# An encoder on one core: the weights' hi parts moved from 64 to 192 bytes past a multiple of 256, and the v projection in 256-column products

## The chip, the core and the metric

The kernel runs on one core of a Trainium2 chip. The metric is the time on the device in microseconds (us), the median of several executions. The core has engines that work side by side: TensorE (PE in the profile, and PEld for its weight loads) multiplies a stationary operand of 128x128 with a moving operand of up to 512 columns and adds into PSUM; VectorE (DVE) and ScalarE (ACT) work elementwise; SyncE (SP) issues the transfers from memory (HBM) into the on-chip memory (SBUF). SBUF has 128 partitions; a byte offset below is always an offset within a partition.

## The reference

Two encoder layers on 256 tokens of width 2048, in float32. The first mixes tokens by a gated short convolution, the second by attention with three groups of dilated windows; each is followed by a gated MLP of width 5632 with a convolution of width 3. Cut to what matters:

```
for i in range(2):
    h = rmsnorm(x, mix_norm_g[i])
    x = x + (short_conv_mixer(h, ...) if i == 0 else dilated_attention_mixer(h, ...))
    h = rmsnorm(x, ffn_norm_g[i])
    u = dwconv3(h @ w_up, conv_w, conv_b)      # 2048 -> 2 * 5632
    a, b = split(u, 2)
    x = x + (silu(a) * b) @ w_down             # 5632 -> 2048
return rmsnorm(x, final_norm_g)

# attention: qkv = h @ w_qkv, 3 groups x (q, k, v) x 16 heads x 128;
# per group softmax(q k^T / sqrt(128) - slope * distance) v, the groups mixed by their denominators
```

Nearly all of the work is in the products with weight matrices: 2048 x 6144 and 2048 x 2048 in the first mixer, 2048 x 18432 and 2048 x 2048 in attention, 2048 x 11264 and 5632 x 2048 in each MLP.

## The kernel before

**Products in two parts.** PE multiplies in a rounded float32 form (F32R). To keep float32's accuracy, each operand is split into a hi part, the rounded value, and a lo part, the rest: `split` (L80) lets ACT copy the source into hi and DVE subtract hi from the source into lo. A product of two split operands is hi·hi + hi·lo + lo·hi. An activation tile (`h`, `a`, `y`, `o`) holds 512 columns per block of 128 channels: 256 tokens of hi (T = 256), then 256 tokens of lo.

**Most products** have the weights as the stationary operand. `mm` (L102) issues two products per block k: L108 multiplies the weights' hi part with all 512 columns of the activation, and L109 the weights' lo part with the 256 hi columns. The results stand in a PSUM tile of 512 columns, whose halves are added afterwards (`gathered`, L117). PE loads the stationary operand anew for every product, so such a pair has two loads: hi for L108, lo for L109. `mm1` (L98) is the same for the first weights of the program, `last` (L245) for the last projection's end; its last output block takes three products of 256 columns instead (L254 to L256), which all add into the same 256 columns.

**The weight tile.** `load_w` (L86) has SP load up to 16 blocks of 128x128 into `raw`, and splits them eight at a time into a tile `w2` of W2 columns; four such tiles are in turn. Where the hi and the lo part begin in it is set by the constants at the top, in elements of 4 bytes:

```
W2 = 2 * 8 * P + 64
HI = 16
LO = 8 * P + 64
LOV = 0
LOS = 9 * P + 64
HIV = 4 * 2 * P + 16
```

P is 128. HI and LO are for `load_w`, HI and LOS for the first weights in `short_conv` (L204), LOV and HIV for the v units. A `w2` tile is 8448 bytes, 33 x 256, and the pools lay every weight tile, every raw tile and the activations at a multiple of 256 bytes. So the hi parts begin 64 bytes past a multiple of 256 (16 elements), the lo parts at a multiple (LO is 4352 bytes, LOV 0). Only the small tiles of the pool "temps" (`tmp`, `e`, `sq`) lie 64 past one, by a spare tile of TPAD elements ahead of them.

**The v units** (`v_unit`, L361) have it the other way round: the activations `h` are stationary, and the weights move, 256 output channels (two heads) at a time. For each block k and each half i of the tokens there were two products: L380 multiplies the hi part of `h` with 512 columns, which an access pattern `both` collects from 256 columns of the weights' lo part and 256 of their hi part, and L381 multiplies the lo part of `h` with the weights' hi part and adds it to the second half of the PSUM tile. For `both` the two parts must lie as far apart (HIV) as half of the pattern's length. At the end of a unit ACT scales the first half into `tmp` (L389), and DVE scales the second half and adds `tmp` (L391). There are 24 v units, each with 16 blocks and 2 halves: 768 pairs.

**The order of work.** The stages follow one another: the short convolution (48 + 720 pairs for its first projection, 256 for its second), the first MLP (88 units of 16 pairs for w_up, and 64 units of 11 for w_down, chunk by chunk), attention, the second MLP. In attention, for each two heads, there are three v units, then twelve q/k units (`qk_unit`, 16 pairs each, 1536 in all), and between these units one waiting task at a time of earlier heads: scores (L413 to L415, L427), softmax, transposes (L446) and the products with v (L464, L469). The order of instructions on each engine is that of the code; a planner adds the semaphores. Four PSUM tiles of 512 columns are in turn, so PE can go on while ACT and DVE empty a finished one.

Of the kernel before, what the change touches and what calls it, by code (L numbers as in the profile page):

```python
# [10 lines left out]
F32 = mybir.dt.float32  # L11
F32R = mybir.dt.float32r
AF = mybir.ActivationFunctionType
ALU = mybir.AluOpType
AX = mybir.AxisListType

P = 128
T = 256
D = 2048
KT = D // P  # L20
# [10 lines left out]
TPAD = 16  # L31

W2 = 2 * 8 * P + 64
HI = 16
LO = 8 * P + 64
LOV = 0
LOS = 9 * P + 64
HIV = 4 * 2 * P + 16
QSCALE = float(P) ** -0.5


# [1 line left out]
def encoder_kernel(ctx: ExitStack, tc: tile.TileContext, xT, gs, scw, fcw, dist, w_first, w_in, w_so, w_v, w_qk, w_ao, w_up, w_dn, out):  # L43
# [3 lines left out]
    pe, dve, act = nc.tensor, nc.vector, nc.scalar  # L47
# [3 lines left out]
    tp = ctx.enter_context(tc.tile_pool(name="temps", bufs=2))  # L51
# [5 lines left out]
    rc = cp.tile([P, 2], F32, name="rc")  # L57
    x = cp.tile([P, KT, T], F32, name="x")
    h = cp.tile([P, KT, 2 * T], F32R, name="h")
# [20 lines left out]
    def split(hi, lo, src):  # L80
        ins = act.copy(hi, src)  # L81
        dve.tensor_sub(lo, src, f32(hi))  # L82
        return ins


    def load_w(src, n):  # L86
# [3 lines left out]
        for k0 in range(0, n, 8):  # L90
            m = min(8, n - k0)
            w2 = wp.tile([P, W2], F32R, name="w2", tag="w2", bufs=4)
            hi, lo = (w2[:, z : z + 8 * P].rearrange("p (k c) -> p k c", k=8) for z in (HI, LO))
            split(hi[:, :m, :], lo[:, :m, :], raw[:, k0 : k0 + m, :])
# [19 lines left out]
    def new_ps():  # L114
        return pp.tile([P, 2 * T], F32, name="ps", tag="ps", bufs=4)
# [66 lines left out]
    def short_conv():  # L182
        with tc.tile_pool(name="sc", bufs=1) as sp:
# [13 lines left out]
            for n in (1, 1, 2, 2, 3, 3, 2, 1, 1):  # L197
# [6 lines left out]
                w2 = sp.tile([P, LOS + 9 * P], F32R, name="w2s", tag="w2s", bufs=2)  # L204
                w2 = [w2[:, z : z + 9 * P].rearrange("p (k c) -> p k c", k=3) for z in (HI, LOS)]
                ins = split(w2[0][:, :n, :], w2[1][:, :n, :], raw[:, :n, :])
# [134 lines left out]
    def attention():  # L341
        with tc.tile_pool(name="att", bufs=1) as sp:
# [9 lines left out]
            def norms():  # L352
                rms()
                dve.tensor_copy(rp.rearrange("p (i m) -> p i m", i=2), rr.rearrange("p (m i) -> p i m", i=2))
                dve.tensor_scalar_mul(rq, rp, QSCALE)
                for i in range(2):
                    ps = pp.tile([P, 2 * T], F32, name="stat", tag="s", bufs=2)
                    pe.transpose(ps[:, :P], rp[:, i * P : (i + 1) * P], ident)
                    dve.tensor_copy(rc[:, i : i + 1], ps[:, 0:1])

            def v_unit(hp, g):  # L361

                first = hp == 0 and g == 0
                if g == 0:
                    v = sp.tile([P, 2, 2, T], F32R, name="v", tag="v0", bufs=2)
                else:
                    v = sp.tile([P, 2, T], F32, name="v", tag=f"v{g}", bufs=2)
                ps = [new_ps(), new_ps()]
                for k0 in range(0, KT, 8):
                    raw = wp.tile([P, 8, T], F32, name="rawv", tag="raw", bufs=RAW)  # L370
                    nc.sync.dma_start(raw, w_v[3 * hp + g, :, k0 * T : (k0 + 8) * T])
                    for k1 in range(k0, k0 + 8, 4):
                        w2 = wp.tile([P, W2], F32R, name="w2v", tag="w2", bufs=4)
                        lo, hi = (w2[:, z : z + 4 * T].rearrange("p (k c) -> p k c", k=4) for z in (LOV, HIV))
                        split(hi, lo, raw[:, k1 - k0 : k1 - k0 + 4, :])
                        both = w2[:, : 2 * HIV].rearrange("p (z c) -> p z c", z=2)
                        for k in range(k1, k1 + 4):
                            c = (k - k1) * T
                            for i in range(2):
                                pe.matmul(ps[i], h[:, k, i * P : (i + 1) * P], both[:, :, c : c + T], start=k == 0, stop=False)  # L380
                                pe.matmul(  # L381
                                    ps[i][:, T:], h[:, k, T + i * P : T + (i + 1) * P], hi[:, k - k1, :],
                                    start=False, stop=k == KT - 1,
                                )
                if first:
                    norms()
                for i in range(2):
                    tmp = tp.tile([P, T], F32, name="tmp", tag="tmp")
                    act.mul(tmp, ps[i][:, :T], rc[:, i : i + 1])  # L389
                    e = tp.tile([P, T], F32, name="e", tag="e0") if g == 0 else v[:, i, :]  # L390
                    dve.scalar_tensor_tensor(e, ps[i][:, T:], rc[:, i : i + 1], tmp, op0=ALU.mult, op1=ALU.add)  # L391
                    if g == 0:
                        split(v[:, i, 0, :], v[:, i, 1, :], e)
                vs[hp, g] = v
# [85 lines left out]
            for hp in range(H // 2):  # L480
                for g in range(G):
                    v_unit(hp, g)
                    step()
                for hd in (2 * hp, 2 * hp + 1):
                    for g in range(G):
                        qk_unit(hd, g, 0)
                        step()
                        qk_unit(hd, g, 1)
                        step()
                        tasks.append(lambda hd=hd, g=g: scores(hd, g))  # L490
                    tasks.append(lambda hd=hd: (softmax(hd, 0), softmax(hd, 1)))
                    tasks.append(lambda hd=hd: transposes(hd, 0))
                    tasks.append(lambda hd=hd: transposes(hd, 1))
                    tasks.append(lambda hd=hd: pv(hd))
            first = []
            for j in range(2):
                w = load_w(w_ao[j], KT)
                ps = new_ps()
# [5 lines left out]
            for j in range(KT):  # L504
                if j < 2:
                    ps, w = first[j]
                    mm(ps, w, o, range(KT - 1, KT))
                else:
                    w = load_w(w_ao[j], KT)
                    ps = new_ps()  # L510
# [90 lines left out]
```

## Time and profile before

| | |
|---|---|
| median of three runs | 2794.36 us |
| the three runs | 2794.18, 2794.36, 2823.95 us |
| the profiled execution: its own time | 2770.87 us |
| its span, first to last instruction | 2768.8 us |
| mean granted TensorE clock | 0.999 |
| DMA, share of 16 engines (SP's queue) | 53.1% |
| read from HBM | 514.76 MB, 187 GB/s over the span |

In a row of groups one reads the line of the kernel, the engine, the operation, output<-inputs by the program's names, the sizes and the count; behind the bar the busy time in us, the mean duration of one in ns, and the time that the engine was idle just before them with what ended it. PE's durations overlap, since a matmul's end is modelled and the next one starts before it; what one matmul really takes of PE's time is the distance from its start to the next start. A row of the timeline has the start in us, the duration in us, and then the same names. A row of the windows has the window, its length, the busy time of each engine with the count in parentheses, the granted TensorE clock, the DMA share and GB/s.

### The profile page before, as it was taken

What the parts mean: (1) busy time and instruction counts of PE and PEld (TensorE: products, weight loads), DVE (VectorE), ACT (ScalarE), POOL (GpSimd) and SP (SyncE); (2) the same over time, 40 slices, a digit from 0 to 9 for tenths busy, and PEclk for the clock granted to TensorE, in tenths of its full rate; (3) what the DMA queues carried; (4) which work ended last, traced back from release to release, by engine and by line L of the source; (5) the groups of instructions that cost most, each with busy time, mean ns of one, the idle gap of its engine ahead of it and who ended that gap; (6) DMA issues with size and microseconds to landing.
All of it is one profiled execution on the core that took longest, in us unless ns stands there. A gap on an engine that the chain in (4) does not pass through costs nothing.

```text
span 2768.8 us, 40538 instructions
## 1 busy us (share of the span) xinstructions
PE 2750.9 (99%) x16223; PEld 2432.0 (88%) x16223; DVE 1995.9 (72%) x3080; ACT 1502.1 (54%) x2335; POOL 0.7 (0%) x6
## 2 busy tenths in 40 slices
PE   9999999999999999999999999999999999999998
PEld 7888888888888888888888888888888888888887
DVE  7777788877868868655665666566788886877866
ACT  6454566655655556444444444444566655655655
POOL 0000000000000000000000000000000000000000
PEclk9999999999999999999999999999999999999999
DMA  7555555546555456544545454545455546556554
GB/s 251 207 188 197 198 188 193 198 167 215 191 183 210 171 189 221 186 177 168 182 171 176 171 182 168 177 173 179 171 195 189 195 170 220 189 176 218 177 183 144
DMA packets 79821, 519.48 MB, mean 188 GB/s; under 512 B 9104, under 2 KB 10256, under 8 KB 28816
## 3 DMA queue, kind: packets, MB, share of 16 engines
q1 hardware_dynamic: 79488, 516.37, 53.1%
q8 instruction: 127, 2.08, 0.3%
q14 instruction: 62, 0.51, 0.1%
q10 hardware_dynamic: 144, 0.52, 0.0%
HBM read 514.76 MB, written 2.10 MB: 187 GB/s over the span
## 4 chain that ended last, share of the span: by engine, by line
PE 99%; DMA 1%; DVE 0%; ACT 0%; SPq 0%; issue 0%; DVEq 0%; ACTq 0%
PE ps L108 57%; PE ps L109 29%; PE ps L380 6%; PE ps L381 3%; PE ot L469 1%; PE s L427 1%; PE pt L446 1%; PE ot L464 0%; DMA raw<-in_w_first 0%; DMA raw<-in_w_in 0%; DVE x L288 0%; PE s L415 0%; PE s L413 0%; PE s L414 0%; DVE w2s L82 0%; PE stat L169 0%
## 5 line engine op out<-in xcount | busy, mean ns | idle before, releaser
L108 PE MATMUL ps<-h,w 128*128 128x512 f32 x5072 | 1748.6, 392 | 0.3 <-ACT w L81 0.3
L109 PE MATMUL ps<-h,w 128*128 128x256 f32 x5072 | 1406.8, 277 | 0.0
L82 DVE TENSOR_TENSOR w<-raw,w 128x1024 fp32r<-128x1024 f32 (+1 forms) x954 | 1080.7, 1133 | 359.3 <-ACT w L81 341.7
L81 ACT CAST w<-raw 128x1024 fp32r<-128x1024 f32 (+1 forms) x954 | 934.7, 980 | 523.9 <-PE ps L109 420.4
L108 PEld LDWEIGHTS ps<-h,w 128*128 128x128 f32 x5072 | 952.2, 188 | 200.3 <-ACT w L81 0.6
L109 PEld LDWEIGHTS ps<-h,w 128*128 128x128 f32 x5072 | 954.7, 188 | 0.7 <-DVE w L82 0.6
L108 PE MATMUL ps<-a,w 128*128 128x512 f32 x1397 | 475.3, 389 | 0.0
L119 ACT COPY tmp<-ps 128x256 f32<-128x256 f32 x479 | 177.5, 371 | 471.1 <-PE ps L109 471.1
L109 PE MATMUL ps<-a,w 128*128 128x256 f32 x1397 | 385.6, 276 | 0.0
L121 DVE TENSOR_TENSOR e<-ps,tmp 128x256 f32<-128x256 f32 x479 | 201.9, 422 | 228.4 <-ACT tmp L119 228.4
L108 PEld LDWEIGHTS ps<-a,w 128*128 128x128 f32 x1397 | 262.2, 188 | 54.5
L380 PE MATMUL ps<-w2v,h 128*128 128x512 f32 x768 | 270.4, 396 | 0.0
L109 PEld LDWEIGHTS ps<-a,w 128*128 128x128 f32 x1397 | 262.2, 188 | 0.0
L381 PE MATMUL ps<-w2v,h 128*128 128x256 f32 x768 | 213.3, 278 | 0.0
L82 DVE TENSOR_TENSOR w2v<-rawv,w2v 128x1024 fp32r<-128x1024 f32 x96 | 117.5, 1224 | 99.8 <-ACT w2v L81 99.0
L380 PEld LDWEIGHTS ps<-w2v,h 128*128 128x128 f32 x768 | 144.1, 188 | 33.6
L81 ACT CAST w2v<-rawv 128x1024 fp32r<-128x1024 f32 x96 | 100.6, 1048 | 98.2 <-PE ps L381 69.8
L381 PEld LDWEIGHTS ps<-w2v,h 128*128 128x128 f32 x768 | 144.3, 188 | 0.0
L133 ACT ACTIVATE cv<-e,fcw_sb 128x256 f32<-128x256 f32 x176 | 105.7, 602 | 12.1 <-DVE e L128 11.9
L128 DVE TENSOR_TENSOR e<-e,rr 128x256 f32<-128x256 f32 x220 | 92.9, 424 | 6.8
L134 DVE SCALAR_TENSOR_TENSOR cv<-e,fcw_sb,cv 128x255 f32<-128x255 f32 x176 | 84.1, 479 | 8.0 <-ACT cv L133 8.0
L135 DVE SCALAR_TENSOR_TENSOR cv<-e,fcw_sb,cv 128x255 f32<-128x255 f32 x176 | 85.1, 484 | 6.1
(120 smaller groups left out, 1467.9 us busy)
## 6 DMA issues: line engine op xcount, KB each, us to landing
raw<-in_w_up SPq DMA_DIRECT2D x176, 1024.0 KB, 4.7
raw<-in_w_qk SPq DMA_DIRECT2D x96, 1024.0 KB, 4.7
raw<-in_w_dn SPq DMA_DIRECT2D x128, 704.0 KB, 4.0
rawv<-in_w_v SPq DMA_DIRECT2D x48, 1024.0 KB, 5.1
raw<-in_w_in SPq DMA_DIRECT2D x45, 1024.0 KB, 4.8
raw<-in_w_so SPq DMA_DIRECT2D x16, 1024.0 KB, 4.7
raw<-in_w_ao SPq DMA_DIRECT2D x16, 1024.0 KB, 4.8
raw<-in_w_first SPq DMA_DIRECT2D x3, 384.0 KB, 5.7
```

The lines of the kernel that those rows point to most:

```text
L81: ins = act.copy(hi, src)
L82: dve.tensor_sub(lo, src, f32(hi))
L108: pe.matmul(ps, hi[:, i, :], a[:, k, :], start=k == 0, stop=False)
L109: ins = pe.matmul(ps[:, :T], lo[:, i, :], a[:, k, :T], start=False, stop=k == n - 1)
L119: act.copy(tmp, ps[:, T:])
L121: dve.tensor_add(e, ps[:, :T], tmp)
L128: dve.tensor_mul(e, g, r)
L133: act.activation(c, e, AF.Identity, bias=w[:, 3:4], scale=w[:, 1:2])
L134: dve.scalar_tensor_tensor(c[:, 1:], e[:, : T - 1], w[:, 0:1], c[:, 1:], op0=ALU.mult, op1=ALU.add)
L135: dve.scalar_tensor_tensor(c[:, : T - 1], e[:, 1:], w[:, 2:3], c[:, : T - 1], op0=ALU.mult, op1=ALU.add)
L380: pe.matmul(ps[i], h[:, k, i * P : (i + 1) * P], both[:, :, c : c + T], start=k == 0, stop=False)
L381: pe.matmul(ps[i][:, T:], h[:, k, T + i * P : T + (i + 1) * P], hi[:, k - k1, :], start=False, stop=k == KT - 1,)
```

## The change

The hi parts in all weight tiles begin at element 48 in place of 16, which is 192 bytes past a multiple of 256; the lo parts of `load_w` and of the first weights stay at a multiple. In the v units' tiles the lo part begins at element 16 (64 bytes) and the hi part at 192 bytes past a multiple. The pattern `both` is gone: for each block and half there are three products of 256 columns, `h` hi with the weights' hi, `h` hi with the weights' lo, `h` lo with the weights' hi, all into the first 256 columns of the PSUM tile. The scaling at the end writes the result in one ACT operation, and DVE's scaling and sum fall away.

```
-HI = 16
+HI = 48
 LO = 8 * P + 64
-LOV = 0
 LOS = 9 * P + 64
-HIV = 4 * 2 * P + 16
+LOV = 16
+HIV = 4 * 2 * P + 48
...
-                        both = w2[:, : 2 * HIV].rearrange("p (z c) -> p z c", z=2)
                         for k in range(k1, k1 + 4):
-                            c = (k - k1) * T
                             for i in range(2):
-                                pe.matmul(ps[i], h[:, k, i * P : (i + 1) * P], both[:, :, c : c + T], start=k == 0, stop=False)
-                                pe.matmul(
-                                    ps[i][:, T:], h[:, k, T + i * P : T + (i + 1) * P], hi[:, k - k1, :],
-                                    start=False, stop=k == KT - 1,
-                                )
+                                a, b = (h[:, k, z + i * P : z + (i + 1) * P] for z in (0, T))
+                                pe.matmul(ps[i][:, :T], a, hi[:, k - k1, :], start=k == 0, stop=False)
+                                pe.matmul(ps[i][:, :T], a, lo[:, k - k1, :], start=False, stop=False)
+                                pe.matmul(ps[i][:, :T], b, hi[:, k - k1, :], start=False, stop=k == KT - 1)
                 if first:
                     norms()
                 for i in range(2):
-                    tmp = tp.tile([P, T], F32, name="tmp", tag="tmp")
-                    act.mul(tmp, ps[i][:, :T], rc[:, i : i + 1])
                     e = tp.tile([P, T], F32, name="e", tag="e0") if g == 0 else v[:, i, :]
-                    dve.scalar_tensor_tensor(e, ps[i][:, T:], rc[:, i : i + 1], tmp, op0=ALU.mult, op1=ALU.add)
+                    act.mul(e, ps[i][:, :T], rc[:, i : i + 1])
                     if g == 0:
                         split(v[:, i, 0, :], v[:, i, 1, :], e)
```

## The prediction

> **What bounds the kernel now.** I read the page first (busy shares, then the chain that ended last), then the groups by line with shapes kept apart, then the timeline of PE inside single units, because a busy PE is no measure of PE's pace. The page:
>
> ```profile
> PE 2750.9 (99%) x16223; PEld 2432.0 (88%) x16223; DVE 1995.9 (72%) x3080; ACT 1502.1 (54%) x2335; POOL 0.7 (0%) x6
> PE 99%; DMA 1%; DVE 0%; ACT 0%; SPq 0%; issue 0%; DVEq 0%; ACTq 0%
> L108 PE MATMUL ps<-h,w 128*128 128x512 f32 x5072 | 1748.6, 392 | 0.3 <-ACT w L81 0.3
> L109 PE MATMUL ps<-h,w 128*128 128x256 f32 x5072 | 1406.8, 277 | 0.0
> L380 PE MATMUL ps<-w2v,h 128*128 128x512 f32 x768 | 270.4, 396 | 0.0
> L381 PE MATMUL ps<-w2v,h 128*128 128x256 f32 x768 | 213.3, 278 | 0.0
> ```
>
> PE holds 99% of the chain and waited 0.3 us in its largest group, so the time is the number of matmuls times the distance between their starts (the "slot"; the durations in the rows overlap and can't be added). Starts come from the timeline, the counts from the windows. First a stretch of the first MLP, then a q/k unit, a v unit and the end of the last projection:
>
> ```profile
> 499.73 0.28 PE L109 MATMUL ps<-h,w 128*128 128x256 f32 x1
> 599.69 0.28 PE L109 MATMUL ps<-h,w 128*128 128x256 f32 x1
> 500.00:600.00 100.00, 81.15 (x295) 55.22 (x295) 1.00 0.51 184
> ...
> 1142.81 0.40 PE L108 MATMUL ps<-h,w 128*128 128x512 f32 x1
> 1152.96 0.39 PE L108 MATMUL ps<-h,w 128*128 128x512 f32 x1
> 1143.00:1153.00 10.00, 10.00 (x30) 5.41 (x29) 1.00 0.48 152
> ...
> 1208.91 0.39 PE L380 MATMUL ps<-w2v,h 128*128 128x512 f32 x1
> 1218.69 0.39 PE L380 MATMUL ps<-w2v,h 128*128 128x512 f32 x1
> 1209.00:1219.00 10.00, 10.00 (x29) 5.32 (x29) 1.00 0.43 140
> ...
> 2751.79 0.28 PE L254 MATMUL ps<-a,w 128*128 128x256 f32 x1
> 2755.32 0.28 PE L254 MATMUL ps<-a,w 128*128 128x256 f32 x1
> L254 PE MATMUL ps<-a,w 128*128 128x256 f32 x11 | 3.1, 282 | 0.0
> ```
>
> Each block is a first start, a last start and a count (a window's count takes in the one that began just ahead of it, so distances are one fewer). MLP: 294 pairs of a 512- and a 256-column product in 99.96 us, 340 ns a pair. The q/k unit: 29 pairs in 10.15 us, 350 ns, though line, shapes and addresses in the weight tile are the same as in the MLP and the granted clock is 1.00 in both. The v unit: 28 pairs in 9.78 us, 349 ns. Three 256-column products in a row (L254 to L256): 10 triples in 3.53 us, 353 ns. All four stream 768 columns. So the same work runs in a quick rhythm (340) or a slow one (350). The groups by window tell the rhythms apart by duration:
>
> ```profile
> L108 PE MATMUL ps<-h,w 128*128 128x512 f32 x1386 | 471.4, 389 | 0.0
> L109 PE MATMUL ps<-h,w 128*128 128x256 f32 x1387 | 382.8, 276 | 0.0
> ...
> L108 PE MATMUL ps<-h,w 128*128 128x512 f32 x1536 | 544.0, 397 | 0.0
> L109 PE MATMUL ps<-h,w 128*128 128x256 f32 x1536 | 430.3, 280 | 0.0
> ```
>
> The first two rows are the second MLP (2045 to 2751 us), 389 and 276 ns; the last two the attention stage (1079 to 1964 us), 397 and 280. In this execution both MLPs kept the quick rhythm and attention mostly had the slow one.
>
> **The profiled execution and the median.** The profiled execution took 2770.87 us, 2.1 over its span; the timed runs were 2794.18, 2794.36 and 2823.95. The steps, 23 and 53 us, fit the two rhythms: an MLP has 2112 pairs (88 units of 16, 64 of 11), and 10 ns on each is 21 us; both MLPs and the first mixer's 976 pairs are 52 us. That is an estimate; only the profiled execution can be looked into. I therefore make the sum against 2770.87 and add 23.5 for the median.
>
> **The change, part by part.** *v units.* 768 times a 512-column product and a 256-column one become three of 256. Columns are the same; 768 matmuls and 768 weight loads are added. Before: 349 ns. After, by the nearest row (the triple, whose weights lie at both 0 and 64 bytes past 256): 353 ns, so 768 x 4 = +3 us. Bounds: if each ran like the 256-column slot of the quick rhythm, a third of 340 (340 is three equal parts by columns), the triple is 340 and the unit gains 768 x 9 = 7 us. The dearest 256-column triple is the scores' (L413 to L415):
>
> ```profile
> L413 PE MATMUL s<-qk 128*128 128x256 f32 x32 | 9.0, 283 | 0.0
> L415 PE MATMUL s<-qk 128*128 128x256 f32 x32 | 9.1, 284 | 0.0
> L464 PE MATMUL ot<-pT,v 128*128 128x256 f32 x96 | 14.3, 283 | 0.0
> ```
>
> That is 1 to 2 ns a product over L254, at most 6 ns a triple on top of the 4: 768 x 10 = +8 us. I take +3, since L254 to L256 repeat one triple 11 times without a break, as the v unit will. The added weight loads hide under the products: in the triples each already has one.
>
> *The v unit's end.* The ACT scaling stays (now written straight into e); the DVE operation behind it goes, and with it the sum of two halves:
>
> ```profile
> L389 ACT ACTIVATE tmp<-ps,rc 128x256 f32<-128x256 f32 x48 | 20.1, 470 | 33.2 <-PE ps L381 31.0 <-DVE rc L359 2.1
> L391 DVE SCALAR_TENSOR_TENSOR v<-ps,rc,tmp 128x256 f32<-128x256 f32 x32 | 14.0, 479 | 9.8 <-ACT tmp L389 9.8
> ```
>
> 48 x 0.48 us leave DVE (23 us of 1996), and v is ready 0.48 us sooner. No PE row waits for it, so I count nothing; PE's matmuls cover it, and if that cover were gone it could be a gain of 23 us at most, not a loss.
>
> *The offsets on ACT and DVE.* All splits (L81, L82) now write and read the hi part at 192. If an offset mattered to these engines it would show between the same split on tiles with different remainders: `e` lies 64 past a multiple of 256, the MLP's `cv` at a multiple.
>
> ```profile
> L81 ACT CAST qk<-e 128x256 fp32r<-128x256 f32 x32 | 13.1, 408 | 1.9 <-DVE e L128 1.9
> L81 ACT CAST a<-cv 128x256 fp32r<-128x256 f32 x88 | 35.9, 408 | 18.1 <-DVE cv L313 17.5
> L82 DVE TENSOR_TENSOR qk<-e,qk 128x256 fp32r<-128x256 f32 x32 | 13.4, 418 | 0.0
> L82 DVE TENSOR_TENSOR a<-cv,a 128x256 fp32r<-128x256 f32 x88 | 36.8, 418 | 0.0
> L82 DVE TENSOR_TENSOR w<-raw,w 128x1024 fp32r<-128x1024 f32 x826 | 1010.6, 1224 | 359.3 <-ACT w L81 341.7
> ```
>
> 408 against 408 and 418 against 418: nothing. If 192 did cost there, DVE has 28% idle, and the 826 large weight splits could each grow by about 0.9 us on average (773 us idle over 826) before DVE took over as the bound. Zero.
>
> *The offsets on PE.* This is the large unknown: while a product streams, the next one's weights are loaded, and every second load of the 6981 L108/L109 pairs now starts at 192 instead of 64. Loads from 0 and from 64 stand in the trace: in the quick rhythm both are free (276 and 389 ns), and a 256-column product in the slow rhythm takes 281 to 284 ns whether its neighbours' weights lie at 0 (L413, L464) or partly at 64 (L254). By these the remainder does not set the pace; what does is how PE left the last interruption. Lower bound: all pairs quick; upper bound: all slow (the rivals). I take zero.
>
> [...]
>
> Sum: 2770.87 + 3 = 2774 for an execution like the profiled one, and 2773.9 + 23.5 = 2797 for the median.
>
> **The rivals.** *Faster: the slow rhythm goes.* If loads from 192 no longer meet the stream, the slow rhythm may be impossible. Then at most 1536 q/k pairs gain 10 ns (15 us; a few are quick already), about 100 pairs at the start 1 us, and the v units 7 us: 2771 - 23 = 2748 whatever the luck, 1.7% under the median. For it: two rhythms at one set of addresses show that PE's loads and streams do disturb each other. Against it: the loads of the lo part stay at 0 under the 512-column product, and moving the load from 0 to 64 shows no difference. If the v units alone gained, 2770.87 - 7 + 23.5 = 2787: no change. A pace below 340 has no row, so I leave it out.
>
> *Slower: the quick rhythm goes.* In the v units the load lies 192 past the streamed hi part (0 against 64), which is the relation that the L109 product now gets, and the v units, at 349, never settle at 340. If that is the cause, all pairs take 350: 976 + 4213 + 256 pairs outside q/k, x 10 ns = 54, so 2771 + 54 + 3 = 2828, 1.2% over the median. It decides by itself once some 90% of those pairs are slow (48 of the 54 us). Against it: the v units differ in more (a 512-column stream in two pieces).
>
> *The change does nothing and the rhythm's luck decides:* 2774, 2797 or 2827, as the three old values plus 3. This is the forecast's own range.
>
> **How the numbers follow.** Forecast (no effect of the address): 0.45, with its own range of 2774 to 2827. Slow rhythm gone: 0.30. Quick rhythm gone: 0.25. About 1% is what a measurement of this kernel can tell from no change; faster by more is below 2766, slower above 2822. The first rival lands below 2766 nearly always (0.28 of 0.30), the second above 2822 mostly (0.20 of 0.25), the forecast's worst luck adds 0.04. So faster 0.28, same 0.48, slower 0.24. The range from 2748 to 2828 takes in both rivals and their bounds, with 3 us beyond each for the v units.
>
> **What would show it.** Forecast: second-MLP rows still 389 and 276 (or 393 and 281 in a slow execution), the three v rows at 281 ns and triples at 353, L81 and L82 at 1.05 and 1.22 us, no L391. First rival: attention's L108 and L109 also at 389 and 276, a v triple at 340. Second: 393 or more and 281 in both MLPs, in every execution. The forecast is wrong at its root if a rhythm appears that is neither 340 nor 350, or if PE begins to wait for L82.

## The result, and the profile after

| | before | after |
|---|---|---|
| median of 19 runs each | 2799.83 us | 2767.20 us |
| the lower group of runs | 2793.9 to 2799.8 (10) | 2765.2 to 2768.1 (11) |
| the upper group of runs | 2823.2 to 2825.3 (9) | 2788.1 to 2789.7 (8) |
| the profiled execution | 2770.87 us | 2788.26 us |

The ratio after to before is 0.9882, with a 95% interval of 0.9849 to 0.9915: 1.2% faster, where no change was forecast. Both kernels have two groups of run times; the median before is the highest run of its lower group, whose other nine lie below 2795.2. The profiled execution of the changed kernel fell into its upper group, and that of the kernel before lay below both of its groups, so the two spans must not be compared as they are. They are compared stage by stage.

The pace of the MLPs, by the windows view: two windows of 400 us, one in each MLP, with the products of L108 alone (the count of pairs stands behind PE's busy time). First the kernel before, then the changed one:

```profile
500.00:900.00 400.00, 400.00 (x1177) 220.81 (x1177) 1.00 0.55 194
2200.00:2600.00 400.00, 400.00 (x1178) 220.77 (x1177) 1.00 0.55 194
```

```profile
500.00:900.00 400.00, 400.00 (x1177) 220.79 (x1177) 1.00 0.56 195
2200.00:2600.00 400.00, 400.00 (x1144) 214.88 (x1143) 1.00 0.54 189
```

400 us over 1177 is 340 ns a pair, over 1144 it is 350. The first MLP is alike; the changed kernel's second MLP ran in the slow rhythm in this execution. 2112 pairs by 10 ns are 21 us: take them off, with 1.9 for w_ao just ahead (256 pairs at 349 ns by their starts, 341 before), and 2788.3 becomes 2765.4, the foot of the lower group. So the changed kernel's lower group is taken as "both MLPs quick". For the kernel before, "both MLPs quick" is the profiled 2770.87, which none of its 19 timed runs reached; by the differences its lower group would have some 23 us, its upper one some 53 us of slow pairs on top. No trace of those runs exists, so that is an estimate; the trace of v_only below, at 2805.75 us, does show such a stretch.

With both MLPs quick the kernels differ by 5.4 us. The timeline gives the place: the first v product and the first product of w_ao, before and after.

```profile
1079.20 0.40 PE L380 MATMUL ps<-w2v,h 128*128 128x512 f32 x1
1945.72 0.39 PE L108 MATMUL ps<-o,w 128*128 128x512 f32 x1
```

```profile
1078.24 0.28 PE L379 MATMUL ps<-w2v,h 128*128 128x256 f32 x1
1940.27 0.39 PE L108 MATMUL ps<-o,w 128*128 128x512 f32 x1
```

Attention took 866.5 us and takes 862.0: 4.5 less; the other 1.0 had been won by its start. Inside attention two things pull apart. The v units got dearer (timeline and window, L379 alone):

```profile
1208.99 0.28 PE L379 MATMUL ps<-w2v,h 128*128 128x256 f32 x1
1216.76 0.28 PE L379 MATMUL ps<-w2v,h 128*128 128x256 f32 x1
1209.00:1217.00 8.00, 6.38 (x23) 4.18 (x23) 1.00 0.43 142
```

22 triples in 7.77 us are 353 ns, against 349 before: 768 x 4 = +3 us. The q/k units must then have won between 7 and 8 us. Their rows, 397 and 280 ns before, are now nearer to the quick ones:

```profile
L108 PE MATMUL ps<-h,w 128*128 128x512 f32 x1536 | 536.1, 394 | 0.0
L109 PE MATMUL ps<-h,w 128*128 128x256 f32 x1536 | 426.3, 278 | 0.0
```

How they do it stands in the timeline around the four score products of 128 columns that interrupt them (L427 before, L422 after):

```profile
1142.02 0.60 PE L427 MATMUL s<-qkf 128*128 128x128 f32 x4
1142.81 0.40 PE L108 MATMUL ps<-h,w 128*128 128x512 f32 x1
1143.16 0.39 PE L108 MATMUL ps<-h,w 128*128 128x512 f32 x1
1143.51 0.40 PE L108 MATMUL ps<-h,w 128*128 128x512 f32 x1
1143.86 0.39 PE L108 MATMUL ps<-h,w 128*128 128x512 f32 x1
```

```profile
1141.64 0.60 PE L422 MATMUL s<-qkf 128*128 128x128 f32 x4
1142.43 0.40 PE L108 MATMUL ps<-h,w 128*128 128x512 f32 x1
1142.78 0.39 PE L108 MATMUL ps<-h,w 128*128 128x512 f32 x1
1143.13 0.39 PE L108 MATMUL ps<-h,w 128*128 128x512 f32 x1
1143.47 0.39 PE L108 MATMUL ps<-h,w 128*128 128x512 f32 x1
1143.81 0.39 PE L108 MATMUL ps<-h,w 128*128 128x512 f32 x1
```

Before, the pairs stay 0.35 us apart until the next interruption. After, they are 0.35 apart twice and then 0.34: PE falls back into the quick rhythm. The kernel before could do that as well, behind another interruption, the score products of 256 columns (L413 to L415) just ahead of 1131.12 us:

```profile
1131.12 0.40 PE L108 MATMUL ps<-h,w 128*128 128x512 f32 x1
1131.47 0.39 PE L108 MATMUL ps<-h,w 128*128 128x512 f32 x1
1131.82 0.39 PE L108 MATMUL ps<-h,w 128*128 128x512 f32 x1
1132.16 0.39 PE L108 MATMUL ps<-h,w 128*128 128x512 f32 x1
```

So what changed is how often. Of the q/k pairs that follow each other without a break, 16% start 342 ns or less apart before, and 66% after.

### The profile page after: what moved, and what is told of

It reads as the page before. It is cut to its first block, busy times and chain, and to the rows that moved or that the text cites. A ratio compares the mean times of both kernels' runs of the same rounds, so it can differ in the third digit from the quotient of the medians.

```text
span 2786.2 us, 41986 instructions
## 1 busy us (share of the span) xinstructions
PE 2768.5 (99%) x16991; PEld 2476.5 (89%) x16991; DVE 1978.2 (71%) x3032; ACT 1504.0 (54%) x2335; POOL 0.7 (0%) x6
## 4 chain that ended last, share of the span: by engine, by line
PE 98%; DVE 1%; DMA 0%; ACT 0%; issue 0%; SPq 0%; DVEq 0%; ACTq 0%
PE ps L108 57%; PE ps L109 29%; PE ps L380 3%; PE ps L379 3%; PE ps L381 3%; PE ot L464 1%; PE s L422 1%; PE pt L441 1%; PE ot L459 0%; DMA raw<-in_w_first 0%; PE ps L99 0%; DVE x L288 0%; PE s L408 0%; PE s L410 0%; PE s L409 0%; PE ps L100 0%
## 5 line engine op out<-in xcount | busy, mean ns | idle before, releaser
L108 PE MATMUL ps<-h,w 128*128 128x512 f32 x5072 | 1754.2, 392 | 0.0
L109 PE MATMUL ps<-h,w 128*128 128x256 f32 x5072 | 1409.0, 278 | 0.1
L108 PEld LDWEIGHTS ps<-h,w 128*128 128x128 f32 x5072 | 952.7, 188 | 203.5
L109 PEld LDWEIGHTS ps<-h,w 128*128 128x128 f32 x5072 | 952.4, 188 | 1.0 <-DVE w L82 0.8
L108 PE MATMUL ps<-a,w 128*128 128x512 f32 x1397 | 482.2, 392 | 0.0
L109 PE MATMUL ps<-a,w 128*128 128x256 f32 x1397 | 388.7, 278 | 0.0
L108 PEld LDWEIGHTS ps<-a,w 128*128 128x128 f32 x1397 | 262.4, 188 | 57.7
L109 PEld LDWEIGHTS ps<-a,w 128*128 128x128 f32 x1397 | 262.2, 188 | 0.0
L379 PE MATMUL ps<-w2v,h 128*128 128x256 f32 x768 | 216.5, 282 | 0.0
L380 PE MATMUL ps<-w2v,h 128*128 128x256 f32 x768 | 216.2, 282 | 0.0
L381 PE MATMUL ps<-w2v,h 128*128 128x256 f32 x768 | 215.0, 280 | 0.0
L82 DVE TENSOR_TENSOR w2v<-rawv,w2v 128x1024 fp32r<-128x1024 f32 x96 | 117.5, 1224 | 103.5 <-ACT w2v L81 102.6
L381 PEld LDWEIGHTS ps<-w2v,h 128*128 128x128 f32 x768 | 145.3, 189 | 0.0
L380 PEld LDWEIGHTS ps<-w2v,h 128*128 128x128 f32 x768 | 144.3, 188 | 0.0
L379 PEld LDWEIGHTS ps<-w2v,h 128*128 128x128 f32 x768 | 144.1, 188 | 0.1
```

Source lines behind the costliest of these rows:

```text
L108: pe.matmul(ps, hi[:, i, :], a[:, k, :], start=k == 0, stop=False)
L109: ins = pe.matmul(ps[:, :T], lo[:, i, :], a[:, k, :T], start=False, stop=k == n - 1)
L379: pe.matmul(ps[i][:, :T], a, hi[:, k - k1, :], start=k == 0, stop=False)
L380: pe.matmul(ps[i][:, :T], a, lo[:, k - k1, :], start=False, stop=False)
L381: pe.matmul(ps[i][:, :T], b, hi[:, k - k1, :], start=False, stop=k == KT - 1)
```

## The experiments

The theory that the traces suggest, A: a product streams while the next product's weights load; in a pair the hi load of the next block runs under the 256-column product, and the lo load under the 512-column one. The timeline of the kernel before shows both, a product and the next load at the same time or 0.01 us apart:

```profile
1000.21 0.28 PE L109 MATMUL ps<-a,w 128*128 128x256 f32 x1
1000.21 0.19 PEld L108 LDWEIGHTS ps<-a,w 128*128 128x128 f32 x1
1000.32 0.39 PE L108 MATMUL ps<-a,w 128*128 128x512 f32 x1
1000.33 0.19 PEld L109 LDWEIGHTS ps<-a,w 128*128 128x128 f32 x1
```

By A the place of that load modulo 256 decides whether PE can leave the slow rhythm. Rival B: the offset is of no account, and the other length of the v units merely shifts the moments at which PE starts again.

### One part at a time

```
# hi192_only: before with       # v_only: the changed kernel with
-HI = 16                        -HI = 48
+HI = 48                        +HI = 16
```

> The kernel before with HI = 48 alone (v units as they were). Theory A (address): a weight load that starts at 192 lets PE fall back into the quick rhythm after an interruption, so this part carries the gain: executions at about 2761 or 2784 us (the changed kernel's two values less 4 for its dearer v units), and the q/k pairs of attention mostly at 340 ns (L108 389 to 392 ns, L109 276 to 278). Theory B (phase): only the changed length of the v units shifts the moments at which PE starts again; then this kernel runs as the one before, 2794 or 2824, with q/k pairs at 350.

> The change without its first line: HI stays 16, v units in 256-column products at 192 and 64. Theory A: no gain, the v units cost 3 to 4 us more, 2798 or 2828 us, q/k pairs still at 350 ns. Theory B: this part carries the gain, 2765 or 2789, and the MLPs are quick more often.

Measured: hi192_only 2761.29 us, all six runs between 2760.5 and 2764.6, against 2812.77 for the kernel before beside it (26 runs, in groups at 2801 and 2824): ratio 0.9804 (0.9771 to 0.9838), so whether it is a full 2% stays open. Against the lower group alone it is 40 us. v_only had runs at 2804 to 2806 and at 2828 to 2831, median 2828.73, ratio 1.0017 (0.9984 to 1.005). Windows of hi192_only, then of v_only:

```profile
500.00:900.00 400.00, 400.00 (x1177) 220.78 (x1177) 1.00 0.56 195
2200.00:2600.00 400.00, 400.00 (x1178) 220.77 (x1177) 1.00 0.55 195
```

```profile
500.00:900.00 400.00, 400.00 (x1144) 214.70 (x1143) 1.00 0.54 187
2200.00:2600.00 400.00, 400.00 (x1177) 220.81 (x1177) 1.00 0.56 193
```

A foretold 2761 and had it; B falls. The q/k pairs are mostly quick (78% start 342 ns or less apart, and the row of L109 stands at 277 ns, 280 before), though with the interrupted ones in it the row of L108 stands at 394 ns and not at the 389 to 392 foretold. For v_only A gave 2798 or 2828, and it had 2805 and 2829, 4 to 6 us over the kernel before's groups beside it. So the whole gain is the offset's, and the v units cost 4 us: 2761.3 without their change, 2765.4 in the changed kernel's lower group. v_only's trace has the slow rhythm in the first MLP (350 ns) and attention (398 and 281 ns in its rows of L108 and L109), and the quick one in the second MLP (340 ns). That its first mixer was slow too is an estimate from the time: 2805.75 - 2765.4, less 21 for the first MLP and 8 for the q/k units, leaves 11 us, and 976 pairs by 10 ns are 10. In its strict form A does not hold: the kernel before leaves the slow rhythm too (at 1131 us, above), only less often, and the changed kernel, with its hi load at 192, kept 350 ns for its whole second MLP.

### Other places of the hi load

```
# hi128_only        # hi0_only
-HI = 16            -HI = 16
+HI = 32            +HI = 0
```

> The kernel before with HI = 32 (128 bytes past a multiple of 256). Theory A: the pace after interruptions differs again, in one direction or the other by 10 us or more, and the share of quick q/k pairs differs from both 64 and 192. Theory B: 2794 or 2824 as before, q/k pairs at 350.

> The kernel before with HI = 0: hi and lo parts both at a multiple of 256. Theory A: differs from before by 10 us or more; if it is the relation to the streamed columns (at 0) that hurts, it is slower, up to 2830 or beyond. Theory B: 2794 or 2824 as before.

Measured: hi128_only 2839.57 us (nine runs, 2838.7 to 2840.2), ratio 1.0087 (1.0055 to 1.0118); hi0_only 2812.03 (twelve runs, at 2808 to 2810 and 2814 to 2816), ratio 0.9999 (0.9973 to 1.0025). The windows, hi128_only first:

```profile
500.00:900.00 400.00, 400.00 (x1137) 213.60 (x1137) 1.00 0.54 187
2200.00:2600.00 400.00, 400.00 (x1138) 213.70 (x1137) 1.00 0.53 187
```

```profile
500.00:900.00 400.00, 400.00 (x1155) 215.75 (x1155) 1.00 0.54 190
2200.00:2600.00 400.00, 400.00 (x1155) 216.35 (x1154) 1.00 0.55 190
```

A window's count takes in the pair that began just ahead, so 1155 stands for 1154 distances. That is 352 ns a pair with the load at 128 in both MLPs, 347 at 0. For hi0_only the time alone would have misled: its median equals that of the kernel before, and A's "10 us or more" was missed, yet neither 340 nor 350 occurs in its windows. It has two paces of its own: its first mixer ran at 353 ns a pair.

```profile
100.00:270.00 170.00, 170.00 (x482) 90.38 (x481) 1.00 0.52 186
```

### Is it the load's own place, or its place against the stream?

```
# all_plus64: hi192_only, with h, raw and weight tiles 64 bytes further on
+    cp.tile([P, TPAD], F32, name="padh")
     h = cp.tile([P, KT, 2 * T], F32R, name="h")
...
-    tp.tile([P, TPAD], F32, name="padt", tag="padt", bufs=1)
```

> The kernel before with HI = 48, and h, the raw and the weight tiles all 64 bytes further on (a spare tile ahead of h, the one ahead of the temps left out), so that in tile h's products the hi load starts at 0, the lo load at 64 and the stream at 64; a, y and o stay at 0. Theory C (relation): what counts is where the load lies against the streamed columns, modulo 256: h's products (w_up, q/k) have the relations of hi192_only (192 and 0) and stay at 340 ns, 389 and 276 in the rows, while a's and o's products have the new relations 0 and 64 and change. Theory D (place): what counts is the load's own remainder; then h's products run as in hi0_only, which has its hi loads at 0 too, 345 to 353 ns, in every stage, and the time is 2800 to 2820.

Measured: 2771.82 us (four runs, 2770.8 to 2772.6), ratio 0.9867 (0.9819 to 0.9914). Groups by form between 370 and 1080 us, the first MLP (the lines of `mm` are one higher):

```profile
L109 PE MATMUL ps<-h,w 128*128 128x512 f32 x1389 | 472.4, 389 | 0.0
L110 PE MATMUL ps<-h,w 128*128 128x256 f32 x1389 | 383.6, 276 | 0.0
L109 PE MATMUL ps<-a,w 128*128 128x512 f32 x687 | 238.3, 392 | 0.0
L110 PE MATMUL ps<-a,w 128*128 128x256 f32 x686 | 191.9, 280 | 0.0
```

The weights of both groups lie in the same tiles, hi at 0 and lo at 64. Where the stream comes from h, shifted along with them, the durations are the quick ones, 389 and 276; where it comes from a, which stayed at a multiple of 256, they are 392 and 280. By their starts that is 340 and 347 ns a pair (1389 by 340 and 687 by 347 make 711 us, and the window has 710). So the relation counts (theory C), not the load's own remainder (D); nor can it be the writes of ACT and DVE into the weight tiles, whose places are the same for both. Only this one shift, by 64 bytes, was run. The ten microseconds over hi192_only fit the streams left behind (a, y and o): some 1900 pairs by 7 ns are 13 us, and the q/k units, 89% quick here (row of L110 in attention 277 ns), give about 2 back.

### The other load of the pair

```
# lo192_hi192: HI = 48 and      # lo64_hi192: lo part first in the tile
-LO = 8 * P + 64                -HI = 16
+LO = 8 * P + 48                +HI = 8 * P + 48
                                -LO = 8 * P + 64
                                +LO = 16          # lo128_hi192: LO = 32
```

> The kernel before with HI = 48 and the lo parts at 192 too (LO = 8 * P + 48). If only the load under the 256-column product (hi) matters, it runs as hi192_only: 2761 us, pairs at 340 ns. If the load under the 512-column product (lo) matters as well, the pair gets slower (theory C: any lo relation other than 0 may bring the slow rhythm back, 2785 to 2830), or quicker than 340 if 0 was the worse place: then under 2761.

> hi192_only with the two parts exchanged in the tile, the lo part at 64 past a multiple of 256 and the hi part at 192 (the first weights unchanged). Theory C (relation of load and stream): the load under the 512-column product now stands at 64. lo at 0 gave 340 ns a pair, lo at 192 gave 353; if the place of this load counts by itself, 64 lies between: above 2761 and below 2847. If the exchange of the two parts in the tile mattered and not the remainder, 2761 again. Under 340 ns would mean that 0 was not the best place.

> The same with the lo part at 128. Theory C: as for the hi part, 128 is a bad place, pairs at 350 ns or more, 2800 to 2850. If 2761, the lo part's place is of no account and lo192_hi192 was slow because both parts lay at the same remainder.

Measured: lo192_hi192 2846.86 us, ratio 1.0133 (1.0084 to 1.0182); lo64_hi192 2815.96, ratio 1.0075 (1.0044 to 1.0106); lo128_hi192 2802.97, ratio 1.0027 (0.9998 to 1.0055). The last two ratios are to the kernel before's runs up to 2801.6 us alone, the others above to both of its groups; by the times, all three are 40 us or more slower than hi192_only. The load under the 512-column product counts as well, and beside a hi load at 192 only 0 is good for it (340 ns a pair, against 347 at 64 and 128 and 353 at 192). For lo128_hi192 the time foretold came (2800 to 2850), the pace did not: its pairs took 347 ns, not 350 or more. The window of lo192_hi192 in the first MLP:

```profile
500.00:900.00 400.00, 400.00 (x1133) 212.82 (x1133) 1.00 0.54 187
```

That is 353 ns a pair. All places that were run, by the same window (for all_plus64 by the starts of a's pairs):

| hi load, against the stream | lo load, against the stream | ns a pair, first MLP | kernel |
|---|---|---|---|
| 64 | 0 | 340 or 350 | before, v_only |
| 192 | 0 | 340 | hi192_only, the changed kernel |
| 128 | 0 | 352 | hi128_only |
| 0 | 0 | 347 | hi0_only |
| 0 | 64 | 347 | all_plus64, products of a |
| 192 | 192 | 353 | lo192_hi192 |
| 192 | 64 | 347 | lo64_hi192 |
| 192 | 128 | 347 | lo128_hi192 |

Three rows stand for one of two paces: the changed kernel's second MLP ran at 350 and the first mixer of hi0_only at 353. That of lo64_hi192 fits 353 too, an estimate: its MLPs have the pace of hi0_only's, 347, and its profiled span, 2813.0 us, is within 1 us of that one's, 2813.9.

### The v units' places

```
# v256_old_offsets: the changed kernel with   # v_both64, v_both192, v_lo0_hi128: hi192_only with
-LOV = 16                                     -LOV = 0
+LOV = 0                                      +LOV = 16                # 48; 0
-HIV = 4 * 2 * P + 48                         +HIV = 4 * 2 * P + 16    # + 48; + 32
+HIV = 4 * 2 * P + 16                         +both = w2[:, LOV : LOV + 2 * (HIV - LOV)]...
```

> The changed kernel (HI = 48, three 256-column products in the v units) with the v units' parts at the old places, lo at 0 and hi at 64. If these offsets matter there, the v triple leaves 353 to 356 ns by 3 ns or more (2 us in all); if three 256-column products are bound by their loads whatever the place, 2765 us again, or 2788 in an execution with a slow second MLP.

> hi192_only with the v units' 512- and 256-column products as before, lo and hi parts both at 64 past a multiple of 256 (lo at 64, hi at 4160 bytes), so that h's loads, at 0, stand 192 past the streamed columns under both products. If the relation 192 is what makes a pair quick, the v pair falls from 349 toward 340 ns and the time to 2754; if the v units are held by something else (the stream in two pieces), 349 and 2761 again.

> hi192_only with the v units' parts both at 192 past a multiple of 256, so that h's loads, at 0, stand 64 past the streamed columns. If v units are held by what the pairs are held by, their pair moves by some ns from 349 (64 was the mixed place: 340 or 350); if by the stream in two pieces, 349 stays. Time 2761, give or take 7, or 23 more where the second MLP starts in the slow rhythm.

> hi192_only with the v units' lo part at 0 and hi part at 128: the loads under the 256-column product stand 128 past the stream, the relation that was slow everywhere in hi128_only (352 ns a pair). Theory C: the v pair goes up from 349 to 352 or more, the time to 2763 or more, or 23 above that with a slow second MLP.

Measured medians: 2790.20, 2786.59, 2766.13 and 2767.13 us, each with runs in two groups, 2764 to 2769 and 2786 to 2791. As the group of a run covers the few microseconds of the v units, I read their pace from the timeline. Two starts and the window of hi192_only, then of v_both64 (L380 alone):

```profile
1207.63 0.39 PE L380 MATMUL ps<-w2v,h 128*128 128x512 f32 x1
1216.34 0.39 PE L380 MATMUL ps<-w2v,h 128*128 128x512 f32 x1
1208.00:1216.50 8.50, 8.50 (x26) 4.55 (x25) 1.00 0.44 151
```

```profile
1207.64 0.39 PE L380 MATMUL ps<-w2v,h 128*128 128x512 f32 x1
1216.46 0.39 PE L380 MATMUL ps<-w2v,h 128*128 128x512 f32 x1
1208.00:1216.50 8.50, 8.50 (x26) 4.54 (x25) 1.00 0.35 126
```

25 pairs in 8.71 us are 348 ns, in 8.82 us 353. By the same reading v_both192 and v_lo0_hi128 have 353 (24 pairs in 8.48 us in each), as foretold for both, and the triples with the old offsets (v256_old_offsets) 356 (22 in 7.84 us) against 353 in the changed kernel, just the 3 ns from which on the place was to count. So the place moves the v units by 3 to 5 ns too, and the pair at 0 and 64, as the kernel before has it, is the best of those run. The hope that the relation 192 under both products would bring 340 (v_both64) was wrong.

Best of all that ran is hi192_only: the first line of the change without the rest.

## Why the prediction was wrong

*What bounds the kernel:* right. PE's pace is the time; its largest wait after is 5.7 us at the start, and DVE and ACT have the durations that they had (the splits, below, 1224 and 1051 ns, 1224 and 1052 before).

*v units, +3 us:* right. The triple was forecast at 353 ns and is 353; hi192_only against the changed kernel's lower group gives 4 us.

*The v units' end, nothing; ACT and DVE offsets, nothing:* right. The splits after, by form, with hi at 192:

```profile
L82 DVE TENSOR_TENSOR w<-raw,w 128x1024 fp32r<-128x1024 f32 x826 | 1011.0, 1224 | 384.1 <-ACT w L81 366.8
L81 ACT CAST w<-raw 128x1024 fp32r<-128x1024 f32 x826 | 867.8, 1051 | 533.9 <-PE ps L109 419.1 <-issue 61.1 <-PE ps L381 33.4
```

*The offsets on PE, "I take zero":* this is the step that failed. Two readings led there. The first, that loads from 0 and from 64 are both free in the quick rhythm, holds only for the two loads as they stood, lo at 0 under the 512-column product and hi at 64 under the 256-column one. Changed singly they are not free: with hi at 0 (hi0_only) a pair takes 347 ns or more, with lo at 64 beside hi at 192 (lo64_hi192) as well. And the reading says what a pair costs once PE is in the quick rhythm, not whether PE finds back into it. The second compared 256-column triples, which take 353 to 356 ns at every place that was run; a stream that is slow anyway can't show what the place does to a pair. What I set against the first rival, that the lo load stays at 0, speaks for it: by lo192_hi192, lo64_hi192 and lo128_hi192, 0 is the only good place for that load beside a hi load at 192. What the prediction put in place of the address, how PE left the last interruption, is a part of it: in the traces of before and after each change of pace, 33 and 36 of them counted by six pairs in a row, comes within four pairs of another product or a wait of PE, and in hi192_only the starts behind the scores at 1140.57 us lie 0.43, 0.35, 0.35 and then 0.34 us apart. But the relation of load and stream decides which paces occur (the table above) and how often the quick one is taken (16% of the q/k pairs before, 66% after). The sign named for being wrong at the root, a rhythm that is neither 340 nor 350, came in the experiments: 347, 352 and 353.

*The luck of the rhythm:* half right. The reading of the run times as an execution with no, one or more slow stretches is borne out by one run of the kernel before beside the experiments, at 2771.28 us. But I carried the median's 23.5 us over as luck that the change would not touch, and these were the larger part of the gain. From the middle of the lower group before (2794.3) to that of the lower group after (2765.8) are 28.5 us: 5.4 are seen in the traces, and the other 23 fit slow pairs that are gone.

*The first rival* was what happened, at a smaller size. It gave 2748: q/k units 15 us less, v units 7 us less, all MLPs quick. The q/k units won 7 to 8, since several pairs pass before the quick rhythm is found and some units stay slow; the v units cost 3 instead; and in 8 of 19 runs one stretch was still slow. *The second rival* (192 as the bad relation) had taken the v units for evidence on the pairs, and 192 is the place where the pairs did best. What holds the v units is not known: none of the variants brought them under 348. Beside a lo load at 0, the slow places of the hi load are 128 (352 ns in both MLPs, and a run 78 us longer than hi192_only's, 11 ns on each of 6981 pairs) and 0 (347 or 353).

With unchanged work and a granted clock of 1.00 a pair of the first MLP took 340 to 353 ns over the places of its loads that were run (the table above).

**What stays open.** That 256 is enough as a period is seen in the kernel itself: the weight tiles, 8448 bytes each, begin by turns at 0 and at 256 past a multiple of 512, and whole MLPs kept one pace (340 ns, 1177 pairs in 400 us). Why the period is 256 bytes, and what slows PE at the other places, was not shown: all_plus64 gives the effect of the relation, 340 against 347 ns, and no cause of it. Nor was it settled why, with the hi load at 192, the second MLP can still start slowly: at 350 ns in the changed kernel's trace and, judged by run times some 22 us apart, in 8 of its 19 runs and some of all four v-unit variants', but in none of hi192_only's six runs and all_plus64's four. In the profiled changed kernel the slow stretch began with w_ao (349 ns a pair). The kernel before's lower group lies at 2794 beside the changed kernel and at 2801 beside most experiments; which stages were slow in each is not known.

## What to carry to other kernels

When PE is the bound and its matmuls come with a weight load each, measure the distance between starts, not durations or busy shares, and look for two distances for the same pair: that may be time to be won without removing any work. Then move the stationary operand against the moving one by 64 bytes at a time, each load of the repeating pattern by itself, and judge by the pace in the trace. Run times in separate groups should be taken apart by stage before two medians are compared, and the parts of a change timed one by one: here half of it earned 40 us or more in its own comparison (51 between the medians) and the other half cost 4.

## What the hardware showed that was not expected

In these traces a stream of unchanged pairs had more than one steady pace at a granted clock of 1.00, and kept it for thousands of products: in the changed kernel's trace the first MLP holds 340 ns from end to end and the second 350, and in the traces of before and after the pace changes only within four pairs of an interruption. The relation of the load's and the stream's addresses modulo 256 went with the paces (340 or 350, 347 or 353, 352) and with how often the quick one was taken (16% of the q/k pairs with the hi load at 64, 66% at 192). None of the windows of 400 us that were read in the MLPs shows less than 340 ns a pair.
